# Where an MLP begins and ends: moved loads and squares, another product order, a scaling placed behind the next sum

## The chip, the cores and the metric

The kernel runs on one core of one Trainium2 chip. The metric is the device time of one execution in microseconds (us). The core's engines are TensorE (PE in the profile; its weight loads are PEld), VectorE (DVE), ScalarE (ACT), GpSimd (POOL) and SyncE (SP). SP, ACT and POOL also issue DMAs.

## The reference

One layer of a hybrid encoder on 512 rows of width 1024, in float32: two kinds of attention, a cross attention, then the part that matters here, an MLP with 4096 hidden columns, and a final normalisation.

```
h = h + concat(fox_out, rec) @ w_out
h = h + memory_cross_attention(rmsnorm(h), rmsnorm(mem), ...)
u = rmsnorm(h) @ w1            # (512, 1024) @ (1024, 4096)
h = h + square(relu(u)) @ w2   # (512, 4096) @ (4096, 1024)
out = rmsnorm(h)
```

## The kernel before

The last part of the kernel is the MLP. Its 4096 hidden columns are cut into 8 groups of 512 (`NG`). Within a group each matrix product, up (`u`, with `w1`) and down (`d`, with `w2`), is a 2 x 2 block product made of seven smaller products instead of eight; they are named "1" to "7". Their inputs are sums and differences of blocks. Only the last down group is done plainly, one block of 128 rows and one half of the columns at a time (`first_half`, steps "y", then `last_block`).

Each float32 operand is split into a high part in a rounded format and a low part that holds the rest, and each product is three matmuls: high x high, high x low, low x high. For weights the split (`prep`, through `split_of`) is one ScalarE instruction (line 163) and one VectorE instruction (line 165) for each block; the results `whu`/`wlu` and `whd`/`wld` live in rings of four buffers, so a split waits until the product four places earlier has been computed.

An up product (`up`) is 24 matmuls of 256 columns. Products "1", "6", "7", "4" add into one PSUM bank (`uU`, a pool with a single buffer), and "2" and "5", "3" into others (`uY`). As the bank is added to again, the running value is copied out to `h` by ScalarE (line 1350) behind "1", "6" and "5"; "7" can't begin to add until "6" is copied, and "1" of the next group can't begin until "4" has been read by its relu (`c`, line 1355). A down product (`down`) is 12 matmuls of 512 columns into the banks `U`, `Y` or `V`, and `add_to` (VectorE, line 1409) adds a finished bank, scaled with the row's factor `r2`, into `acc`, the residual of each block of 128 rows. `r2` comes from `row_scales`: four ScalarE squares of `acc` (128 x 1024 each, `aj`) and three tiny VectorE instructions.

The raw weights are loaded by SP (`load_raw`), block by block, into five slots for up (`uq`, `uk`, `us`) and five for down (`wq`, `dk`), by the roles a1, b1, a2, b2, c1. Sums of raw blocks are made by POOL's adding DMAs (`add_raw`) and, for up's c1, by VectorE. `begin` starts this for group 0, `behind` continues it behind each split.

The order of work: TensorE's instructions stay in the order of the text. The other engines' queues are ordered by a scheduler, which takes what is ready by its own clock, with the order of the text as priority. `tc.keep_in_program_order(x)` pins an instruction behind the one traced before it on its engine. The list `steps` sets which product comes when: all up products, with the down products slipped in from step 7 on; at the end the last down products alternate with the steps "y".

The end: for each of four row blocks, `last_block` makes the second half's products (12 matmuls, the last block's in two pieces), sums them into `acc` (VectorE), squares them (ScalarE, line 1460), makes the row's factor on POOL (`fe`, line 1463, and `fr`, line 1488) and scales the two halves by it, one on ScalarE (line 1489) and one on VectorE (line 1491); then both go out by DMA. `fa` (POOL, line 1486) is the first half multiplied by the final gain ahead of its factor.

Of the kernel before, what the change touches and what calls it, by code (L numbers as in the profile page):

```python
# [12 lines left out]
AF = mybir.ActivationFunctionType  # L13
ALU = mybir.AluOpType
# [3 lines left out]
S = 512  # L18
NT = S // P
D = 1024  # L20
KC = D // P
M = 256
WT = 256
# [4 lines left out]
EPS = 1e-6  # L28
# [14 lines left out]
def emit(  # L43
# [22 lines left out]
    te, ve, ac, gp = nc.tensor, nc.vector, nc.scalar, nc.gpsimd  # L66
# [26 lines left out]
    def s4(shape, name, dt=F32):  # L93
        return s4p.tile([P] + shape, dt, tag="s4", name=name)

    def k4(shape, name, dt=F32):
        return k4p.tile([P] + shape, dt, tag="k4", name=name)

    def q2(name, dt=R):
        return q2p.tile([P, 2, S], dt, tag="q2", name=name)  # L100
# [4 lines left out]
    def t2(name, dt=F32, shape=(S,)):  # L105
        return t2p.tile([P] + list(shape), dt, tag="t2", name=name)

    def sm(n, name):
        if n > 8:
            return s3p.tile([P, n], F32, tag="s3", name=name, padded_shape=[P, 32])  # L110
        return smp.tile([P, n], F32, tag="sm", name=name, padded_shape=[P, 8])

    def mm(name, shape=(S,)):
        return mmp.tile([P] + list(shape), F32, tag="mm", name=name)
# [7 lines left out]
    def tr(name, shape=(S,)):  # L122
        return trp.tile([P] + list(shape), F32, tag="tr", name=name)
# [25 lines left out]
    NG = DFF // HG  # L149
# [174 lines left out]
    mhalf = cp.tile([P, 8], F32, name="mhalf")  # L324
# [36 lines left out]
    for half in range(2):  # L361
        mkf = t2(f"mkf{half}", F32, (6, 64))
        gp.memset(mkf, 1.0)
        for li, m in enumerate(mlev[:-1]):
            v = mkf[:, li, :].rearrange("p (b m) -> p b m", m=m)
            nb = 64 // m
            o = half * m
# [538 lines left out]
    for n in range(len(units) + LAG):  # L906
        if n < len(units):
            p, tb, j = units[n]
# [39 lines left out]
    def hTc(c):  # L948
        return hT[c // 2][:, c % 2, :]
# [122 lines left out]
    acc = []  # L1072

    def to_tok(c):
        ps = tr(f"ht{c}")
        for tb in range(NT):
            te.transpose(ps[:, tb * P : (tb + 1) * P], hTc(c)[:, tb * P : (tb + 1) * P], ident)
        for tb in range(NT):
            d, s_ = acc[tb][:, c * P : (c + 1) * P], ps[:, tb * P : (tb + 1) * P]
            if tb % 2 == 0:  # L1080
                ac.activation(d, s_, AF.Copy)  # L1081
            else:
                ve.tensor_copy(d, s_)
# [100 lines left out]

    units, unit_q, keys = {}, deque(), []
    PRODUCTS = {"u": ("1", "2", "5", "6", "7", "3", "4"), "d": ("1", "2", "6", "5", "7", "3", "4")}
    RAW = {"1": "a1", "2": "b1", "6": "a1", "5": "c1", "7": "a2", "3": "b2", "4": "b1"}
    QUAD = {"a1": (0, 0), "a2": (0, 1), "b2": (1, 1), "b1": (1, 0)}
    slots = {}

    def quadrant(kind, g, role):
        r, c = QUAD[role]
        if kind == "u":
            a = w1[r * S : (r + 1) * S, g * HG + c * HS : g * HG + (c + 1) * HS]
        else:
            a = w2[g * HG + r * HS : g * HG + (r + 1) * HS, c * S : (c + 1) * S]
        return a.rearrange("(k p) n -> p k n", p=P)

    def parts_of(kind):
        return 4 if kind == "u" else 2  # L1200

    def load_raw(kind, g, role, source=None):

        if g >= NG:
            return
        slot = slots[kind, role]
        nc.sync.dma_start(slot.rearrange("p (k n) -> p k n", k=parts_of(kind)), quadrant(kind, g, source or role))

    def add_raw(kind, to, of):
        k = parts_of(kind)  # L1210
        src = of if of is not None and not isinstance(of, str) else slots[kind, of].rearrange("p (k n) -> p k n", k=k)
        gp.dma_start(slots[kind, to].rearrange("p (k n) -> p k n", k=k), src, accum_op=ALU.add)  # L1212

    def seven(kind, g):
        return g < (NG if kind == "u" else NG - 1)

    def first_sums(kind, g):

        if not seven(kind, g):
            return  # L1220
        if kind == "u":
            ve.tensor_tensor(slots[kind, "c1"], slots[kind, "a1"], slots[kind, "a2"], ALU.add)
            add_raw(kind, "a2", "b2")
        else:
            load_raw(kind, g, "c1", "a1")
# [5 lines left out]
    def second_sum(kind, g):  # L1231
        if kind == "d" and seven(kind, g):
            add_raw(kind, "a2", quadrant(kind, g, "b2"))

    def begin(kind):
        for role in ("a1", "b1", "a2", "b2"):
            load_raw(kind, 0, role)
        second_sum(kind, 0)
        first_sums(kind, 0)

    def behind(kind, g, name):

# [18 lines left out]
    def prep(kind, g, name):  # L1261
        raw = slots[kind, RAW[name] if seven(kind, g) else name]
        if seven(kind, g) and name == "4":
# [16 lines left out]
            prep(*unit_q.popleft())  # L1280
        return got

    ups = [("u", g, n) for g in range(NG) for n in PRODUCTS["u"]]
    downs = [("d", g, n) for g in range(NG - 1) for n in PRODUCTS["d"]]
    steps = []
    for i, step in enumerate(ups):
        steps.append(step)
        if i in (7, 9, 10, 12, 13, 15, 16) or i >= 18:
            steps.append(downs.pop(0))
    steps += downs[:2]  # L1290
    for i in range(NT):
        steps += [("y", NG - 1, str(i)), *downs[2 + i : 3 + i]]
    last_keys = [("d", NG - 1, n) for n in ("b1", "a1", "b2", "a2")]
    for key in steps:
        if key[0] != "y":
# [6 lines left out]
    def first_units():  # L1302

        ws = [wrp.tile([P, UK * UW], F32, tag="wr", name=f"us{i}")[:, 0:D] for i in range(2)]
        qs = [q2(f"uq{i}", F32).rearrange("p a b -> p (a b)") for i in range(2)]
        for role, slot in zip(("a1", "b1", "a2", "b2", "c1"), (*qs, k4([D], "uk"), *ws)):
            slots["u", role] = slot
        begin("u")
        for _ in range(2):
            prep(*unit_q.popleft())  # L1310

# [14 lines left out]
    wq = [ap_.tile([P, 4, D], F32, tag="act", name=f"wq{j}") for j in range(2)]  # L1326
    for role, slot in zip(("a1", "b1", "a2", "b2", "c1"), (*[wq[0][:, i, :] for i in range(4)], k4([D], "dk"))):
        slots["d", role] = slot
    begin("d")
    sqs = {(g, j): wq[1][:, g % 2 * 2 + j, :].rearrange("p (i n) -> p i n", i=2) for g in range(NG) for j in range(2)}  # L1330
    comb, hbs, held, banks = {}, {}, {}, {}

# [62 lines left out]

    r2 = cp.tile([P, 2, NT], F32, name="r2")

    def row_scales():
        ms = sm(NT, "ms2")
        for tb in range(NT):  # L1400
            junk = s4([D], f"aj{tb}")
            ac.activation(junk, acc[tb], AF.Square, scale=1.0 / 32.0, accum_out=ms[:, tb : tb + 1])
        ve.tensor_scalar(ms, ms, 1.0, EPS, op0=ALU.mult, op1=ALU.add)
        ve.reciprocal(r2[:, 0, :], ms)
        ve.tensor_scalar(r2[:, 1, :], r2[:, 0, :], -1.0, None, op0=ALU.mult)

    def add_to(ps, tb, cs, sign=1):
# [45 lines left out]
    sums, outs = {}, {}  # L1453
# [17 lines left out]
        if tb < 2:  # L1471
            squares(tb, slice(0, S))

    def last_block(tb, pieces):

        a = acc[tb]
        for n, ns in enumerate(pieces):
            ps = mm(f"y1{tb}_{ns.start}")[:, ns]
            plain_down(ps, tb, 1, ns)
            cs = slice(S + ns.start, S + ns.stop)  # L1480
            add_to(ps, tb, cs)
            squares(tb, cs, n == len(pieces) - 1)
        o, part = outs[tb], sums[tb][-1]
        h0, h1 = slice(0, S), slice(S, D)
        ag = t2(f"fa{tb}")
        gp.tensor_tensor(ag, a[:, h0], gfin[:, h0], op=ALU.mult)
        r = sm(1, f"fr{tb}")
        gp.tensor_tensor(r, part, mhalf[:, 0:1], op=ALU.pow)
        ac.activation(o[:, h0], ag, AF.Identity, scale=r)
        ac.dma_start(out[tb * P : (tb + 1) * P, h0], o[:, h0])  # L1490
        ve.scalar_tensor_tensor(o[:, h1], a[:, h1], r, gfin[:, h1], op0=ALU.mult, op1=ALU.mult)
        nc.sync.dma_start(out[tb * P : (tb + 1) * P, h1], o[:, h1])

    parts = deque()
    for n, (kind, g, name) in enumerate(steps):
        while parts and sum((a, b) in hbs for _, a, b in steps[n:] if _ == "d") < 2:
            hidden_part(*parts.popleft())
        if kind == "y":
            first_half(int(name))
            continue  # L1500
        (up if kind == "u" else down)(g, name)
        if (kind, g, name) == ("u", 0, "1"):
            to_tok(KC - 1)
            row_scales()
        if (kind, g, name) == ("d", NG - 2, "4"):
            while unit_q:
                prep(*unit_q.popleft())
        if (kind, g, name) == ("u", NG - 1, "3"):
            for k in range(2, 4):
                hidden_plain(g, k)  # L1510
        if (kind, name) == ("u", "4"):
            if g < NG - 1:
                parts.extend((g, m) for m in PRODUCTS["d"])
            else:
                for k in range(2):
                    hidden_plain(g, k)
    for tb in range(2, NT):
        squares(tb, slice(0, S))
    gfin = wrp.tile([P, UK * UW], F32, tag="wr", name="gfin")[:, 0:D]
    gp.dma_start(gfin, final_norm_g.partition_broadcast(P))  # L1520
    for tb in range(NT):
        last_block(tb, [slice(0, S)] if tb < NT - 1 else [slice(0, WT), slice(WT, S)])


# [26 lines left out]
```

## Time and profile before

| | |
|---|---|
| median of 3 runs | 783.56 us (782.96 to 784.21) |
| profiled execution, its own time | 782.28 us |
| its span in the profile | 780.4 us |
| TensorE busy | 759.8 us, 97% of the span |
| VectorE, ScalarE, GpSimd busy | 549.8, 432.0, 181.7 us |
| mean granted TensorE clock | 0.993 of full speed |
| MLP's first matmul, last matmul (start) | 445.6 us, 771.54 us |

The span is what the profiler saw from the first to the last instruction; the execution's own time is 1.9 us more. Row starts in the timeline are in us from the span's start, followed by the duration in us, the engine, the line, the operation, output<-input, and in brackets the idle time ahead of it with what ended it. A busy engine is not necessarily the bound, and idle time matters only on the chain that ends last.

### The profile page before, as it was taken

The page shows a single profiled execution, that of the slowest core. Times are in us where ns is not written, and L with a number is a line of the kernel's source. Part 1 is how long each engine was busy: PE and PEld are TensorE (multiplying, and loading weights), DVE is VectorE, ACT ScalarE, POOL GpSimd, SP SyncE. Part 2 cuts the span into 40 slices and gives each one's busy share as a digit, 9 for nine tenths or more (in the row PEclk, how much of TensorE's full clock was granted, in tenths as well). Part 3 has the DMA queues.
Part 4 walks back from the last instruction along what each step waited for, and adds up shares of the span by engine and source line. Part 5 has one row for each costly group of instructions (what it writes and reads, how often), then busy time and mean ns, then how long its engine had stood idle before and what let it go on. Part 6 is the DMA issues. An engine that isn't in the chain of part 4 may idle for free.

```text
span 780.4 us, 12861 instructions
## 1 busy us (share of the span) xinstructions
PE 759.8 (97%) x4940; PEld 672.0 (86%) x4940; DVE 549.8 (70%) x876; ACT 432.0 (55%) x730; POOL 181.7 (23%) x265
## 2 busy tenths in 40 slices
PE   7999999999999999999999989999999999999995
PEld 5889998978989998888888888989999898989874
DVE  3736755687677746645557777859797988888973
ACT  3664555575565533335445586646565656565733
POOL 6105332423433104510000111111112121212022
PEclk8999999999999999999999999999999999999998
DMA  6642332234444353221143789697988888888602
GB/s 194 222 128 80 111 81 56 82 72 119 136 129 142 118 180 105 84 82 55 55 134 108 150 229 198 166 256 172 209 198 230 189 239 189 237 192 168 167 27 109
DMA packets 84223, 113.11 MB, mean 145 GB/s; under 512 B 4881, under 2 KB 62778, under 8 KB 84162
## 3 DMA queue, kind: packets, MB, share of 16 engines
q1 hardware_dynamic: 69890, 74.25, 30.1%
q0 software_dynamic: 11568, 35.15, 23.2%
q10 hardware_dynamic: 2704, 2.89, 1.1%
q8 instruction: 39, 0.64, 0.3%
q14 instruction: 22, 0.18, 0.1%
HBM read 88.14 MB, written 4.21 MB: 118 GB/s over the span
## 4 chain that ended last, share of the span: by engine, by line
PE 90%; DVE 4%; ACT 3%; issue 1%; POOL 1%; DMA 1%; ACTq 0%; POOLq 0%
PE uU L1345 4%; PE uU L1346 4%; PE uU L1347 4%; PE U L1437 3%; PE U L1438 3%; PE U L1439 3%; PE uY L1346 3%; PE uY L1345 3%; PE uY L1347 3%; PE xq L226 2%; PE xw L226 2%; PE xw L228 2%; PE xq L228 2%; PE xq L227 2%; PE xw L227 2%; PE wo L226 2%
## 5 line engine op out<-in xcount | busy, mean ns | idle before, releaser
L163 ACT ACTIVATE whd<-wq 128x1024 fp32r<-128x1024 f32 x39 | 41.3, 1058 | 45.7 <-DMA wq<-wq 15.3
L165 DVE TENSOR_TENSOR wld<-wq,whd 128x1024 fp32r<-128x1024 f32 x39 | 47.6, 1220 | 12.9 <-ACT whd L163 12.8
L1345 PE MATMUL uU<-x2s,whu 128*128 128x256 f32 x160 | 45.9, 287 | 5.2 <-ACT h L1350 3.7
L1347 PE MATMUL uU<-x2s,wlu 128*128 128x256 f32 x160 | 45.3, 283 | 0.0
L1437 PE MATMUL U<-whd,hb 128*128 128x512 f32 x112 | 43.9, 392 | 0.0
L1438 PE MATMUL U<-wld,hb 128*128 128x512 f32 x112 | 43.9, 392 | 0.0
L1439 PE MATMUL U<-whd,hb 128*128 128x512 f32 x112 | 43.6, 389 | 0.0
L1409 DVE SCALAR_TENSOR_TENSOR acc<-U,r,acc 128x512 f32<-128x512 f32 x56 | 40.3, 743 | 4.3 <-PE U L1439 4.2
L163 ACT ACTIVATE whu<-uq 128x1024 fp32r<-128x1024 f32 x28 | 29.6, 1057 | 23.0 <-PE uU L1346 9.6
L165 DVE TENSOR_TENSOR wlu<-uq,whu 128x1024 fp32r<-128x1024 f32 x28 | 34.1, 1219 | 4.8 <-ACT whu L163 4.7
L1345 PEld LDWEIGHTS uU<-x2s,whu 128*128 128x128 f32 x160 | 30.6, 191 | 7.5 <-ACT h L1350 4.1
L1346 PE MATMUL uY<-x2a,whu 128*128 128x256 f32 x128 | 36.2, 283 | 0.0
L1346 PE MATMUL uU<-x2a,whu 128*128 128x256 f32 x128 | 36.2, 283 | 0.0
L1346 PE MATMUL uU<-x2b,whu 128*128 128x256 f32 x128 | 36.2, 283 | 0.0
L1212 POOL DMA_DIRECT2D uk<-us x8 | 8.2, 1026 | 111.1 <-ACT acc L1081 85.7
L163 ACT ACTIVATE whu<-us 128x1024 fp32r<-128x1024 f32 x20 | 21.2, 1060 | 21.1 <-PE uU L1346 16.0
L165 DVE TENSOR_TENSOR wlu<-us,whu 128x1024 fp32r<-128x1024 f32 x20 | 24.4, 1222 | 10.2 <-ACT whu L163 8.6
L847 POOL TENSOR_SCALAR bi<-nF,Ft 128x128 f32<-128x128 f32 (+3 forms) x32 | 21.4, 670 | 42.6 <-PE pt L874 25.1
L1347 PEld LDWEIGHTS uU<-x2s,wlu 128*128 128x128 f32 x160 | 30.6, 191 | 0.0
L864 ACT ACTIVATE bi<-bi,mx 128x128 f32<-128x128 f32 (+3 forms) x32 | 17.9, 559 | 20.9 <-DVE mx L862 20.7
L1345 PE MATMUL uY<-x2s,whu 128*128 128x256 f32 x96 | 27.2, 283 | 0.0
L1347 PE MATMUL uY<-x2s,wlu 128*128 128x256 f32 x96 | 27.2, 283 | 0.0
(944 smaller groups left out, 2826.3 us busy)
## 6 DMA issues: line engine op xcount, KB each, us to landing
wq<-in_w_dram SPq DMA_DIRECT2D x31, 512.0 KB, 5.1
uq<-in_w_dram SPq DMA_DIRECT2D x12, 512.0 KB, 5.0
us<-in_w_dram SPq DMA_DIRECT2D x12, 512.0 KB, 5.9
wq<-wq POOLq DMA_DIRECT2D x11, 512.0 KB, 7.7
wq<-in_w_dram POOLq DMA_DIRECT2D x10, 512.0 KB, 8.9
uk<-in_w_dram SPq DMA_DIRECT2D x8, 512.0 KB, 6.7
dk<-in_w_dram SPq DMA_DIRECT2D x8, 512.0 KB, 4.0
uk<-us POOLq DMA_DIRECT2D x8, 512.0 KB, 6.6
```

The costliest lines, as they stand in the source:

```text
L163: ac.activation(hi, raw, AF.Copy)
L165: ve.tensor_tensor(lo, raw, f(hi), ALU.subtract)
L226: te.matmul(ps, wh, hi, start=n_ == 0, stop=False)
L227: te.matmul(ps, wh, lo, start=False, stop=False)
L228: te.matmul(ps, wl, hi, start=False, stop=n_ == KC - 1)
L1345: te.matmul(ps[:, i, :], whi[:, k, ws], xh, start=first_ and (k, i) == (0, 0), stop=False, skip_group_check=True)
L1346: te.matmul(ps[:, i, :], whi[:, k, ws], xl, start=False, stop=False, skip_group_check=True)
L1347: te.matmul(ps[:, i, :], wlo[:, k, ws], xh, start=False, stop=k == 3, skip_group_check=True)
L1409: ve.scalar_tensor_tensor(a, ps, r2[:, 0 if sign > 0 else 1, tb : tb + 1], a, op0=ALU.mult, op1=ALU.add)
L1437: te.matmul(ps, hi, whi[:, k, :], start=first_ and k == 0, stop=False, skip_group_check=True)
L1438: te.matmul(ps, hi, wlo[:, k, :], start=False, stop=False, skip_group_check=True)
L1439: te.matmul(ps, lo, whi[:, k, :], start=False, stop=k == 1, skip_group_check=True)
```

## The change

- `begin` is cut into three: `a1` and `b1`, then `a2` and `b2`, then the sums. Up calls the three one behind the other as before. Down's, which stood ahead of all products, come one each behind the first three steps.
- The first up group takes its products in the order 1, 2, 6, 5, 7, 3, 4 instead of 1, 2, 5, 6, 7, 3, 4.
- The four row squares come one each behind steps 2 to 5, each pinned behind what was traced before it on ScalarE; the rest of `row_scales` comes behind step 6. Before, all of it came behind step 0.
- Down products are slipped in behind steps 7, 8, 10, 12, 13, 15 and from 17 on, instead of 7, 9, 10, 12, 13, 15, 16 and from 18 on.
- At the end the order y0, "3", y1, "4", y2, y3 becomes y0, y1, "3", y2, "4", y3.
- `last_block` is taken apart. The four `fa` products are traced first. Then each block's sums and squares come ahead of the scaling of the block before it, and its factor behind that; the two scalings are pinned to that place on ScalarE and VectorE.

```diff
+    def products(kind, g):
+        return PRODUCTS["d" if (kind, g) == ("u", 0) else kind]
...
-    def begin(kind):
-        for role in ("a1", "b1", "a2", "b2"):
-            load_raw(kind, 0, role)
-        second_sum(kind, 0)
-        first_sums(kind, 0)
+    def begin(kind, n):
+        if n < 2:
+            for role in (("a1", "b1"), ("a2", "b2"))[n]:
+                load_raw(kind, 0, role)
+        else:
+            second_sum(kind, 0)
+            first_sums(kind, 0)
...
-    ups = [("u", g, n) for g in range(NG) for n in PRODUCTS["u"]]
+    ups = [("u", g, n) for g in range(NG) for n in products("u", g)]
...
-        if i in (7, 9, 10, 12, 13, 15, 16) or i >= 18:
+        if i in (7, 8, 10, 12, 13, 15) or i >= 17:
             steps.append(downs.pop(0))
     steps += downs[:2]
     for i in range(NT):
-        steps += [("y", NG - 1, str(i)), *downs[2 + i : 3 + i]]
+        steps += [("y", NG - 1, str(i)), *(downs[1 + i : 2 + i] if i else ())]
...
-    begin("d")
...
+    def row_squares(tb):
+        junk = s4([D], f"aj{tb}")
+        square = ac.activation(junk, acc[tb], AF.Square, scale=1.0 / 32.0, accum_out=ms2[:, tb : tb + 1])
+        tc.keep_in_program_order(square)
...
-    def last_block(tb, pieces):
+    def last_sums(tb, pieces):
...
+    def last_factor(tb):
+        rs[tb] = sm(1, f"fr{tb}")
+        gp.tensor_tensor(rs[tb], sums[tb][-1], mhalf[:, 0:1], op=ALU.pow)
+
+    def last_scale(tb):
+        o = outs[tb]
+        tc.keep_in_program_order(ac.activation(o[:, h0], ags[tb], AF.Identity, scale=rs[tb]))
         ac.dma_start(out[tb * P : (tb + 1) * P, h0], o[:, h0])
-        ve.scalar_tensor_tensor(o[:, h1], a[:, h1], r, gfin[:, h1], op0=ALU.mult, op1=ALU.mult)
+        tc.keep_in_program_order(ve.scalar_tensor_tensor(o[:, h1], acc[tb][:, h1], rs[tb], gfin[:, h1], op0=ALU.mult, op1=ALU.mult))
...
-        if (kind, g, name) == ("u", 0, "1"):
+        if n < 3:
+            begin("d", n)
+        if n == 0:
             to_tok(KC - 1)
+        if 2 <= n < 6:
+            row_squares(n - 2)
+        if n == 6:
             row_scales()
...
     for tb in range(NT):
-        last_block(tb, [slice(0, S)] if tb < NT - 1 else [slice(0, WT), slice(WT, S)])
+        ags[tb] = t2(f"fa{tb}")
+        gp.tensor_tensor(ags[tb], acc[tb][:, h0], gfin[:, h0], op=ALU.mult)
+    for tb in range(NT):
+        last_sums(tb, [slice(0, S)] if tb < NT - 1 else [slice(0, WT), slice(WT, S)])
+        if tb:
+            last_scale(tb - 1)
+        last_factor(tb)
+    last_scale(NT - 1)
```

More of the change, by code (lines that the diff above doesn't have):

```diff
@@ L1307, in first_units @@
             slots["u", role] = slot
-        begin("u")
+        for n in range(3):
+            begin("u", n)
         for _ in range(2):
@@ L1396, in emit @@
     r2 = cp.tile([P, 2, NT], F32, name="r2")
-    def row_scales():
[L1399 to L1404, printed above, removed]
+    ms2 = sm(NT, "ms2")
+    def row_squares(tb):
+        junk = s4([D], f"aj{tb}")
+        square = ac.activation(junk, acc[tb], AF.Square, scale=1.0 / 32.0, accum_out=ms2[:, tb : tb + 1])
+        tc.keep_in_program_order(square)
+    def row_scales():
+        ve.tensor_scalar(ms2, ms2, 1.0, EPS, op0=ALU.mult, op1=ALU.add)
+        ve.reciprocal(r2[:, 0, :], ms2)
         ve.tensor_scalar(r2[:, 1, :], r2[:, 0, :], -1.0, None, op0=ALU.mult)
@@ L1472, in first_half @@
             squares(tb, slice(0, S))
-    def last_block(tb, pieces):
-        a = acc[tb]
+    def last_sums(tb, pieces):
         for n, ns in enumerate(pieces):
@@ L1482, in last_block @@
             squares(tb, cs, n == len(pieces) - 1)
[L1483 to L1489, printed above, removed]
+    h0, h1 = slice(0, S), slice(S, D)
+    def last_factor(tb):
[4 more added lines that the diff above has]
+        tc.keep_in_program_order(ac.activation(o[:, h0], ags[tb], AF.Identity, scale=rs[tb]))
         ac.dma_start(out[tb * P : (tb + 1) * P, h0], o[:, h0])
-        ve.scalar_tensor_tensor(o[:, h1], a[:, h1], r, gfin[:, h1], op0=ALU.mult, op1=ALU.mult)
+        tc.keep_in_program_order(ve.scalar_tensor_tensor(o[:, h1], acc[tb][:, h1], rs[tb], gfin[:, h1], op0=ALU.mult, op1=ALU.mult))
         nc.sync.dma_start(out[tb * P : (tb + 1) * P, h1], o[:, h1])
@@ L1520, in emit @@
     gp.dma_start(gfin, final_norm_g.partition_broadcast(P))
+    ags, rs = {}, {}
     for tb in range(NT):
-        last_block(tb, [slice(0, S)] if tb < NT - 1 else [slice(0, WT), slice(WT, S)])
+        ags[tb] = t2(f"fa{tb}")
[6 more added lines that the diff above has]
+    last_scale(NT - 1)
 _INS = ['x', 'mem', 'norm_mix_g', 'w_in', 'fox_f_bias', 'hgrn_lb_logits', 'hgrn_norm_g', 'w_out', 'norm_x_g', 'norm_mem_g', 'w_xq', 'w_xkv', 'w_xo', 'norm_ff_g', 'w1', 'w2', 'final_norm_g']
```

## The prediction

> **What bounds the kernel now.** I read the page's busy times first, then TensorE's own waits, then each engine's timeline around those waits.
>
> ```profile
> PE 759.8 (97%) x4940; PEld 672.0 (86%) x4940; DVE 549.8 (70%) x876; ACT 432.0 (55%) x730; POOL 181.7 (23%) x265
> ```
>
> TensorE (PE) is busy for 97% of the span. The change removes no matmul, so it can win only what TensorE loses to waits, and what lies behind its last matmul. TensorE's waits (line, releaser: us in total, times, longest) between 380 and 560 us, and those from 545 us to the end:
>
> ```profile
> PE uU L1345 <- ACT h L1350: 3.7, 2, 2.2
> PE uU L1345 <- ACT c L1355: 1.5, 1, 1.5
> ```
> ```profile
> PE Y L1438 <- DVE wld L165: 1.3, 1, 1.3
> ```
>
> In the whole MLP TensorE waits four times: twice for ScalarE's copy `h`, once for ScalarE's relu `c`, once for VectorE's low weight part `wld`. The tail behind the last matmul is the fifth loss. Each is one term below. A gap is counted from where the next matmul would have started at the usual spacing (0.12 us in an up product, 0.23 us in a down product). A further 0.10 us is an estimate for the first matmul behind each gap: it takes 0.39 instead of 0.28 us in the rows below.
>
> **Term A, the first group's order and the row squares.** TensorE's timeline, then ScalarE's (ACT):
>
> ```profile
> 457.48 0.28 PE L1347 MATMUL uU<-x2b,wlu 128*128 128x256 f32 x1
> 459.93 0.39 PE L1345 MATMUL uU<-x2s,whu 128*128 128x256 f32 x1 [2.18 <-ACT h L1350]
> ```
> ```profile
> 450.77 0.59 ACT L1350 ACTIVATE h<-uU 128x512 f32<-128x512 f32 x1
> ...
> 455.80 1.04 ACT L1402 ACTIVATE aj<-acc 128x1024 f32<-128x1024 f32 x1
> ...
> 458.35 1.04 ACT L163 ACTIVATE whu<-uq 128x1024 fp32r<-128x1024 f32 x1
> 459.30 0.58 ACT L1350 ACTIVATE h<-uU 128x512 f32<-128x512 f32 x1
> ```
>
> Product "6" ended at 457.6, and "7" adds into the same bank, so it waits until "6" is copied out. That copy ran only at 459.30, behind a queue that the four row squares (`aj`; the last at 455.80) had pushed back. The loss is 459.93 - 457.60 = 2.33, with the 0.10 it is 2.43 us. In the new order "5" stands between "6" and "7": 24 matmuls at 0.12 = 2.88 us in another bank, and the copy of "6" has that time. The first square is pinned behind that copy, so no square stands ahead of it. The price of the new order is that "6" starts right behind "2", 24 x 0.12 before 454.72, at 451.84 ("5" ran from there to 454.72), and needs the copy of "1", which ended at 450.77 + 0.59 = 451.36. That leaves 0.48 us, and nothing in the change is put ahead of that copy. I take 2.43, the stall gone. Bounds: 1.39 (one split of 1.04 us ahead of a copy with its cover used up) and 2.43.
>
> The squares aren't removed: four times 1.04 us of ScalarE move into the next products. ScalarE has room there (columns: stretch, length, busy time of PE, PEld, DVE, ACT, POOL, then clock, DMA share, GB/s):
>
> ```profile
> 445.00:461.00 16.00, 13.82 (x115) 13.53 (x114) 11.36 (x22) 14.83 (x27) 1.19 (x1) 1.00 1.02 305
> 461.00:470.00 9.00, 7.83 (x66) 7.62 (x64) 7.25 (x9) 6.62 (x10) 2.25 (x3) 1.00 0.39 75
> ```
>
> ScalarE is full in the first stretch, 14.83 of 16, and has 2.4 us free in the second. The scales made from the squares are wanted only by the first down product's sum, behind "1" of group 1. So the squares cost nothing but in term B; without that cover a square costs its 1.04.
>
> **Term B, from the first group to the second.** "1" of group 1 takes the one bank that "4" of group 0 leaves, and waits for its relu:
>
> ```profile
> 468.55 0.28 PE L1347 MATMUL uU<-x2s,wlu 128*128 128x256 f32 x1
> 470.35 0.39 PE L1345 MATMUL uU<-x2s,whu 128*128 128x256 f32 x1 [1.52 <-ACT c L1355]
> ```
> ```profile
> 468.75 1.06 ACT L163 ACTIVATE whu<-uq 128x1024 fp32r<-128x1024 f32 x1
> 469.71 0.58 ACT L1355 ACTIVATE c<-uU 128x512 f32<-128x512 f32 x1
> ```
>
> It loses 470.35 - 468.67 = 1.68, with 0.10 it is 1.78 us. No product comes between the two after the change either. The floor is the relu alone: the matmuls end at 468.55 + 0.28 = 468.83, the relu takes 0.58, and a hand-over costs 0.06 (469.71 + 0.58 to 470.35) at each end: 469.53, a loss of 0.96 and a gain of 0.82. At the ceiling the last square, pinned behind the square of "3", and a split both stand ahead of the relu: 1.04 worse than now. I take the case between them, the last square a third to run when "4" ends, a loss of 1.3: gain 0.48.
>
> **Term C, the third group.** The new list of steps moves a down product from behind "5" to behind "6" in group 2 (and from "5" to "2" in group 1); from step 18 on both lists put one behind every up product.
>
> ```profile
> 521.18 0.28 PE L1347 MATMUL uU<-x2b,wlu 128*128 128x256 f32 x1
> 522.97 0.39 PE L1345 MATMUL uU<-x2s,whu 128*128 128x256 f32 x1 [1.52 <-ACT h L1350]
> ```
>
> Here too "6" and "7" stood back to back: 522.97 - 521.30 = 1.67, with 0.10 it is 1.77 us. A down product, 12 matmuls at 0.23 = 2.75 us, now covers the copy. Gain 1.77; lower bound 0.73, with a split of 1.04 ahead of the copy.
>
> **The loads of down, later and one by one.** Five loads on SP's queue and one adding load on POOL's move behind loads and sums for the up products of group 1. Now:
>
> ```profile
> 445.28 2.00 SPq L1207 DMA_DIRECT2D wq<-in_w_dram  x4
> ```
> ```profile
> 454.57 1.19 POOL L1212 DMA_DIRECT2D wq<-in_w_dram  x1 [13.58 <-DMA wq<-in_w_dram]
> 463.52 0.89 POOL L1212 DMA_DIRECT2D uk<-us  x1 [7.75 <-DVE wlu L165]
> ...
> 473.81 0.86 POOL L1212 DMA_DIRECT2D us<-uq  x1 [3.42 <-DMA uq<-uk]
> ```
>
> The adding load held POOL's queue for 13.58 us, and the sums of group 1 stand behind it; the first of them (463.52) then waited for VectorE, not for it. With `a2` and `b2` issued behind up's third load, an estimated 4 us later, the adding load moves to about 458.5, still ahead of 463.52. The input of "6" of group 1 is in place at 473.81; its two splits take 1.06 on ScalarE and 1.22 on VectorE (row in term D). That product starts about 467.4 ("1" of group 1) + three up products and two down products, 14.1, at 481.5, so 5 us are left. TensorE has no wait for a DMA now, and I cost this edit at nothing. Bounds: 0, and a loss of 4 if the whole delay came through.
>
> **Term D, plain products sooner.** TensorE, then VectorE (DVE):
>
> ```profile
> 745.37 0.40 PE L1437 MATMUL Y<-whd,hb 128*128 128x512 f32 x1
> 747.11 0.50 PE L1438 MATMUL Y<-wld,hb 128*128 128x512 f32 x1 [1.34 <-DVE wld L165]
> ```
> ```profile
> 745.83 1.22 DVE L165 TENSOR_TENSOR wld<-wq,whd 128x1024 fp32r<-128x1024 f32 x1
> ```
>
> The loss is 747.11 - 745.60 = 1.51, with 0.10 it is 1.61 us. The second plain product, with the same weights and hidden parts as the first, which ran just before, now comes first: 2.75 us, to 748.35, while the split ends at 747.05. Late next are the last two splits, which wait for the buffers that "3" and "4" free, one plain product later than now. "4" would end at 745.60 + 4 x 2.75 = 756.6, its buffer's splits take 2.28, to 758.9, and their weights are read from 756.6 + 1.5 x 2.75 = 760.7. So the gap goes, and none takes its place: 1.61. Bounds: 0 and 1.61.
>
> **Term E, scaling behind the next sum.** The tail, all engines:
>
> ```profile
> 771.54 0.28 PE L1451 MATMUL y<-whd7a,hb 128*128 128x256 f32 x1
> ...
> 772.69 0.75 DVE L1491 SCALAR_TENSOR_TENSOR fo<-acc,fr,gfin 128x512 f32<-128x512 f32 x1 [1.45 <-POOL fr L1488]
> ...
> 773.36 0.48 DVE L1409 SCALAR_TENSOR_TENSOR acc<-y,r,acc 128x256 f32<-128x256 f32 x1
> ...
> 774.54 0.29 POOL L1463 TENSOR_SCALAR fe<-fm,fe 128x1 f32<-128x1 f32 x1 [0.33 <-ACT fo L1460]
> 774.92 0.56 POOL L1488 TENSOR_TENSOR fr<-fe,mhalf 128x1 f32<-128x1 f32 x1
> 775.51 0.72 ACT L1489 ACTIVATE fo<-fa,fr 128x512 f32<-128x512 f32 x1 [1.13 <-POOL fr L1488]
> ```
>
> The matmuls end at T = 771.82, but the last sum ran 1.54 us later, behind the scaling of block 2, which had waited for its own factor. Without that the sum runs at T + 0.06, `fe` 1.18 behind it, `fr` 0.38 behind that, the last scaling 0.59 later: T + 2.21 instead of T + 3.69. Gain 1.48. Block 2's scaling, 0.75, now runs from T + 0.54 to T + 1.29, while ScalarE and POOL make the last factor; without that cover it costs 0.75. Bounds: 0.73 and 1.48.
>
> A VectorE scaling now runs beside POOL's small steps, which it did not before. The same POOL product, first beside a split on VectorE, then alone:
>
> ```profile
> 747.80 2.20 POOL L1486 TENSOR_TENSOR fa<-acc,gfin 128x512 f32<-128x512 f32 x1 [20.74 <-DVE acc L1409]
> 753.72 1.30 POOL L1486 TENSOR_TENSOR fa<-acc,gfin 128x512 f32<-128x512 f32 x1 [3.73 <-DVE acc L1409]
> ```
>
> It took 0.90 us more beside the split. The Trainium skill, "SBUF — State Buffer", section "Who interferes with whom", says that a VectorE instruction with two inputs in SBUF keeps out a GpSimd instruction that reads SBUF; these two rows agree with it. By that rule `fe`, due at T + 1.24, would wait for the scaling's end at T + 1.29, and the sum would be 0.05 us smaller.
>
> **Sum.** 2.43 + 0.48 + 1.77 + 1.61 + 1.48 = 7.77 us. The profiled execution took 782.28 us, so 774.5 by its own time. The median of the runs shown, 783.56, lies 1.28 higher, and the forecast is made against it: 783.56 - 7.77 = 775.8.
>
> **Rivals.**
> 1. The stalls stay in part (chance 0.17). ScalarE's queue is ordered anew, and a split or square of 1.04 us stands ahead of a copy or a relu. For it: such a split stood ahead of the copy in A (458.35) and of the relu in B (468.75). Against it: in A and C the copies get 2.75 to 2.88 us of cover. With nothing gained in B and one further place paid with 1.04 the gain is 6.25: 777.3.
> 2. The front's gain is eaten later (0.09). TensorE comes 4.7 us (A, B, C) earlier, but VectorE, 70% busy over the span, or the loads can't follow. Against it: TensorE has one wait in all behind 545 us, so it is what the others follow. Only D and E stay, 3.1 us: 780.5.
> 3. The tail collides (0.07). Block 2's scaling delays POOL's last factor, or takes VectorE ahead of it, by its whole 0.75: 776.5. It needs that scaling to start late. Its own factor is due at about T - 0.2 (its matmuls end 24 x 0.12 before T; then the chain above, 0.5 longer for the double width), so it can start in time.
> 4. Slower (0.03), by POOL's queue. The adding load waits at its head for the later loads, and the sums of group 1 behind it come too late for "6" of group 1. It takes effect once these sums are 5 us later than now, and the time before is reached another 7.8 us on. The adding load can slip by 9 us before it meets 463.52, so the point is 454.57 + 9 + 12.8 = 476.4. At 479 the time is 786.2. No load in the profile is that late.
>
> That the scheduler issues the loads as early as now would change no term, and belongs to the forecast.
>
> **How the numbers follow.** The forecast has 0.62, a smaller gain of some other kind 0.02. A measurement of this kernel tells 0.2%, some 1.6 us, from no change. The range begins at 774.0 (B at its floor, 0.34 better, and 1.5 for the spread of runs, which is 1.25 in the three shown) and reaches to 779.3, beyond rivals 1 and 3 (0.62 + 0.17 + 0.07 = 0.86) and short of rival 2. Faster takes the forecast and rivals 1 to 3, 0.95, less 0.02 for a rival 2 that takes D and E along; same 0.04, slower 0.03.
>
> **What would show it.** Right: no wait of TensorE for `h` between 445 and 530 us, one of about 1 us for `c` ahead of group 1, none for `wld` near 740, and the last scaling about 2.2 us behind the last matmul. Wrong: a wait for `h` at product "6" (the 0.48 us), a wait for `wq` or a POOL sum between 465 and 500, a new wait between 545 and 735, or the last `fe` later than 1.4 us behind the last matmul.

## The result and the profile after

| | median, us | range | ratio to before, 95% interval |
|---|---|---|---|
| before, same chip | 783.56 | 782.75 to 786.21 (6 runs) | |
| changed | 777.2 | 774.89 to 779.25 (6 runs) | 0.9915 [0.989, 0.9941] |
| profiled execution of the changed kernel | 775.98 | span 774.3 | |

The change makes the kernel 6.4 us faster. The forecast was 775.8, range 774.0 to 779.3. Measured once more, beside the kernel before once more, it took 776.49 against 783.6.

The busy times of the changed kernel, then TensorE's waits from 380 to 560 us and from 545 us to the end (line, releaser: us in total, times, longest):

```profile
PE 758.6 (98%) x4940; PEld 671.2 (87%) x4940; DVE 549.8 (71%) x876; ACT 431.1 (56%) x730; POOL 181.3 (23%) x265
```
```profile
PE uU L1351 <- ACT c L1361: 1.2, 1, 1.2
```
```profile
PE uU L1351 <- ACT c L1361: 2.4, 3, 1.3
```

Both waits for `h` and the one for `wld` are gone. The wait for `c` ahead of group 1 is still there, and three waits for `c` are new in the list. TensorE's timeline of the changed kernel shows all four:

```profile
466.55 0.39 PE L1351 MATMUL uU<-x2s,whu 128*128 128x256 f32 x1 [1.15 <-ACT c L1361]
...
575.14 0.39 PE L1351 MATMUL uU<-x2s,whu 128*128 128x256 f32 x1 [1.27 <-ACT c L1361]
...
615.29 0.39 PE L1351 MATMUL uU<-x2s,whu 128*128 128x256 f32 x1 [0.54 <-ACT c L1361]
...
655.50 0.39 PE L1351 MATMUL uU<-x2s,whu 128*128 128x256 f32 x1 [0.60 <-ACT c L1361]
```

Counted as in the prediction (from where the matmul would have started at the usual spacing, without the extra 0.10), the gaps are 1.31, 1.42, 0.70 and 0.76, together 4.19. Before they were 2.33, 1.68, 1.67 and 1.51, together 7.19.

The tail of the changed kernel, behind its last matmul:

```profile
766.96 0.28 PE L1460 MATMUL y<-whd7a,hb 128*128 128x256 f32 x1
767.28 0.48 DVE L1418 SCALAR_TENSOR_TENSOR acc<-y,r,acc 128x256 f32<-128x256 f32 x1 [0.95 <-PE y L1460]
767.68 0.74 DVE L1501 SCALAR_TENSOR_TENSOR fo<-acc,fr,gfin 128x512 f32<-128x512 f32 x1
...
768.47 0.29 POOL L1472 TENSOR_SCALAR fe<-fm,fe 128x1 f32<-128x1 f32 x1 [1.14 <-ACT fo L1469]
768.85 0.56 POOL L1495 TENSOR_TENSOR fr<-fe,mhalf 128x1 f32<-128x1 f32 x1
...
769.44 0.75 DVE L1501 SCALAR_TENSOR_TENSOR fo<-acc,fr,gfin 128x512 f32<-128x512 f32 x1 [1.02 <-POOL fr L1495]
```

The matmuls end at T = 767.24. The last sum now runs ahead of block 2's scaling, and the last scaling starts at T + 2.20 instead of T + 3.69.

Where the 6.1 us of span went: the MLP's first matmul starts at 444.57 instead of 445.57, so 1.0 us lies ahead of everything the change touches (kernels whose text is the same up to there start it anywhere from 444.57 to 447.19). From that matmul to the last scaling it is 324.87 instead of 329.94 us, a gain of 5.07: 3.00 in gaps, 1.49 in the tail, and 0.58 spread over spacings without a gap of 0.3 us (0.54 of it were three short waits of the kernel before, shown below). The terms A, C, D and E had promised 7.29, and B brought 0.37; the three new waits took 2.88 back, 3.18 with their three slow first matmuls. That leaves 4.48, which is what gaps and tail show (3.00 + 1.49).

### What the new waits are

POOL's timeline of the changed kernel around the group of the second wait. The instructions are adding DMAs; the bracket is the time for which POOL was idle ahead of each:

```profile
543.44 1.21 POOL L1216 DMA_DIRECT2D wq<-in_w_dram  x1 [0.72 <-DMA wq<-in_w_dram]
556.71 1.20 POOL L1216 DMA_DIRECT2D dk<-in_w_dram  x1 [12.06 <-DMA dk<-in_w_dram]
557.44 1.39 POOL L1216 DMA_DIRECT2D wq<-wq  x1
```

ScalarE's timeline behind it:

```profile
567.42 1.06 ACT L163 ACTIVATE whd<-wq 128x1024 fp32r<-128x1024 f32 x1 [5.37 <-DMA wq<-wq]
568.39 1.04 ACT L163 ACTIVATE whu<-uq 128x1024 fp32r<-128x1024 f32 x1
...
573.57 1.04 ACT L163 ACTIVATE whu<-uq 128x1024 fp32r<-128x1024 f32 x1
574.52 0.57 ACT L1361 ACTIVATE c<-uU 128x512 f32<-128x512 f32 x1
```

Down's sum a1 += a2 (`wq<-wq`) is issued at 557.44, directly behind an adding load of c1 (`dk`), for which POOL's queue had stood idle for 12.06 us, until that block's raw load landed. So the sum lands late, and ScalarE, whose next instruction is the split of that sum, idles 5.37 us. From 567.42 on ScalarE works without a pause through what has queued up, and the relu `c` comes at its end, at 574.52. TensorE can't begin the next group until `c` has read the bank.

ScalarE's waits of the kernel before, from 545 to 700 us, and its timeline at the same place, have the same wait (the last row is TensorE's):

```profile
ACT whd L163 <- DMA wq<-wq: 15.3, 4, 4.1
```
```profile
570.83 1.06 ACT L163 ACTIVATE whd<-wq 128x1024 fp32r<-128x1024 f32 x1 [3.21 <-DMA wq<-wq]
...
577.92 0.57 ACT L1355 ACTIVATE c<-uU 128x512 f32<-128x512 f32 x1
```
```profile
579.28 0.28 PE L1345 MATMUL uU<-x2s,whu 128*128 128x256 f32 x1
```

There the relu ended at 578.49 and TensorE wanted the bank at 579.28: a margin of 0.79 us. In the changed kernel TensorE would have arrived at 575.14 - 1.42 = 573.72, 5.56 us earlier, but the sum's split started only 3.41 us earlier (570.83 to 567.42). The difference, 2.15, less the margin of 0.79, is 1.36, and the gap is 1.42.

Ahead of groups 5 to 7 the kernel before had no margin at all. ScalarE's timeline of the kernel before, then TensorE's, with its weight loads (PEld):

```profile
618.07 0.58 ACT L1355 ACTIVATE c<-uU 128x512 f32<-128x512 f32 x1
...
697.11 0.58 ACT L1355 ACTIVATE c<-uU 128x512 f32<-128x512 f32 x1
```
```profile
618.70 0.19 PEld L1345 LDWEIGHTS uU<-x2s,whu 128*128 128x128 f32 x1 [0.35 <-ACT c L1355]
618.70 0.39 PE L1345 MATMUL uU<-x2s,whu 128*128 128x256 f32 x1
...
697.74 0.19 PEld L1345 LDWEIGHTS uU<-x2s,whu 128*128 128x128 f32 x1 [0.41 <-ACT c L1355]
697.74 0.38 PE L1345 MATMUL uU<-x2s,whu 128*128 128x256 f32 x1
```

The relu ends 0.05 us ahead of the matmul, which is no more than a hand-over, and the matmul comes 0.08 and 0.14 us later than the usual spacing and is a slow first one. Ahead of group 6, at 658.17, it is 0.02 late. With 0.10 for each first matmul the three come to 0.54 us. They are too short for the list of waits, which has only `wld` there. So the late sums already set TensorE's pace in these groups, and nothing was left for a TensorE that comes earlier.

### The profile page after: what moved, and what is told of

It reads as the page before. It is cut to its first block, busy times and chain, and to the rows that moved or that the text cites. A ratio compares the mean times of both kernels' runs of the same rounds, so it can differ in the third digit from the quotient of the medians.

```text
span 774.3 us, 12863 instructions
## 1 busy us (share of the span) xinstructions
PE 758.6 (98%) x4940; PEld 671.2 (87%) x4940; DVE 549.8 (71%) x876; ACT 431.1 (56%) x730; POOL 181.3 (23%) x265
```

## The experiments

All are timed in five rounds beside the kernel before on the same chip (783.6 to 784.1). The gaps are TensorE's, read from each timeline.

**1. The changed kernel again, and a pin on POOL's queue.** My theory: the order of POOL's queue makes the new waits. In the text the sum a1 += a2 comes ahead of the adding load of c1; the scheduler had put it behind. The pin keeps the text's order:

```diff
-        gp.dma_start(slots[kind, to]..., src, accum_op=ALU.add)
+        return gp.dma_start(slots[kind, to]..., src, accum_op=ALU.add)
...
-            add_raw(kind, "c1", quadrant(kind, g, "a2"))
+            tc.keep_in_program_order(add_raw(kind, "c1", quadrant(kind, g, "a2")))
```

> The changed kernel once more, unchanged, beside the others of this chip. Its profile showed four waits of TensorE for the relu c, one ahead of group 1 (1.31 us of gap) and three new ones ahead of groups 4, 5 and 6 (1.42, 0.70, 0.76). If these belong to the order of the queues, they stand here again at the same places with sums within 0.5 us, and the time is 775 to 779 us. If they were an accident of one execution, they are elsewhere or gone.

> The changed kernel with one more pin: on POOL, the adding load of c1 from memory stays behind the sum a1 += a2, as in the text, instead of ahead of it. Theory P (POOL's queue): a1 += a2 stood behind the adding load, which waited 12 us for its raw load; so the split of d '6' came late on ScalarE, and the relu behind it. Then a1 += a2 is issued about 5 us earlier (near 552 instead of 557.4), ScalarE's wait for wq<-wq of 4 to 5 us falls to under 1, the three new waits of TensorE go, and the time falls by 2.4 to 3 us against the changed kernel. Theory Q (the DMA engines are full, busy share 0.9 and more in that stage, and the sums land late whatever their order): ScalarE still waits 3 us or more, the waits of TensorE keep at least 2 us in sum, and the time is within 1 us of the changed kernel.

The changed kernel again: 776.49 (775.67 to 778.29), 0.9897 [0.9873, 0.9921]. Its gaps are 1.31 ahead of group 1 and then 0.67, 1.73 and 1.15 at about 537, 617 and 658 us: the new waits stand ahead of groups 3, 5 and 6 instead of 4, 5 and 6, with the same releaser. Together they are 3.55 instead of 2.88, so two of the three places stay, but neither the third nor the sum, which was expected within 0.5. With the pin: 774.09 (772.81 to 774.53), 0.9865 [0.9841, 0.9889]. POOL's timeline of the pinned kernel, then ScalarE's, then TensorE's waits from 380 us to the end:

```profile
542.57 1.21 POOL L1216 DMA_DIRECT2D wq<-in_w_dram  x1 [1.88 <-DMA wq<-in_w_dram]
555.79 0.91 POOL L1216 DMA_DIRECT2D wq<-wq  x1 [12.01 <-DVE wld L165]
556.36 1.58 POOL L1216 DMA_DIRECT2D dk<-in_w_dram  x1
```
```profile
564.41 1.06 ACT L163 ACTIVATE whd<-wq 128x1024 fp32r<-128x1024 f32 x1 [0.62 <-PE U L1448]
...
573.75 0.57 ACT L1361 ACTIVATE c<-uU 128x512 f32<-128x512 f32 x1
```
```profile
PE uU L1351 <- ACT c L1361: 1.2, 1, 1.2
```

The sum now goes first, as soon as VectorE has read the block that it overwrites. Counted from each kernel's first MLP matmul it is issued 3.4 us earlier (555.79 - 446.31 = 109.48 against 557.44 - 444.57 = 112.87). ScalarE's split no longer waits for a DMA but for TensorE, all three new gaps are gone, and only the one ahead of group 1 is left. In every later group the relu now ends 1.12 or 1.13 us before TensorE's matmul. The runs also lie closer together, within 1.7 us instead of 2.6 for the changed kernel on the same chip (4.4 in the first measurement). So the order of POOL's queue is shown to be the cause.

**2. Down's loads put back ahead of all products**, the rest of the change kept. The rival theory was that the later loads make the sums late.

```diff
+    for n in range(3):
+        begin("d", n)
...
-        if n < 3:
-            begin("d", n)
```

> The changed kernel with down's first loads all at once ahead of the products again, as before the change; everything else as changed. Theory L (the later loads put the whole chain of raw sums 2 us later, and this shows as the three new waits): the waits go or halve, and the time falls by 1.5 to 3 us. Theory P: the waits stay, since the order on POOL is the same in the later groups; the time is within 1 us of the changed kernel, and the loads' move is worth nothing by itself.

776.85 (775.86 to 779.33), 0.9905 [0.9881, 0.9928]: as the changed kernel. A gap of 1.74 stands at 576.44, and ScalarE waits four times for the sum, 17.6 us in all. The one new gap is less than the changed kernel's 2.88 and 3.55, as the rival would have it, but the time did not fall by the 1.5 to 3 us that the rival needs, and the sums are as late. Moving the loads neither costs nor brings anything that can be measured here, and the rival falls.

**3. Only the end of the change** (terms D and E: the plain products sooner, and `last_block` taken apart as in the change), with the old front. Against the kernel before, its line in the list of steps is:

```diff
-        steps += [("y", NG - 1, str(i)), *downs[2 + i : 3 + i]]
+        steps += [("y", NG - 1, str(i)), *(downs[1 + i : 2 + i] if i else ())]
```

> Only the end is changed: plain products sooner and the scaling behind the next sum (terms D and E). Loads, squares, product order and list of steps as before the change. By the prediction's terms it gains 1.61 + 1.48 = 3.1 us against the kernel before: 780.5 by its median. The waits for h and c at the front stay as before (3.7 and 1.5 us), and there are no new waits ahead of groups 4 to 6, as the front's stalls give the raw sums their time. Rival: if the new waits came from the end's part of the change, they stand here.

780.95 (778.95 to 784.15, 12 runs), 0.9961 [0.9944, 0.9978], 2.65 us faster. The wait for `wld` is gone, the old front has its old gaps (2.34, 1.68, 1.68), and TensorE's timeline has a new one of 1.50:

```profile
699.75 0.39 PE L1353 MATMUL uU<-x2s,whu 128*128 128x256 f32 x1 [1.34 <-ACT c L1363]
```

That is the wait for `c` again, ahead of group 7, in a kernel whose TensorE comes no earlier; the kernel before had no margin at this place. So the late sums can stop TensorE without the front's gain too; that gain makes the waits likelier and larger, but isn't the whole cause.

This execution also lost some 1.5 us at a place that no term names. Behind the old gap of 2.34 the granted clock fell to 0.50 of full speed, and 16 matmuls came at 0.21 us each instead of 0.12. The kernel before has the same gap without that. Its stretch comes second (columns as in the prediction):

```profile
460.00:462.00 2.00, 2.00 (x11) 2.00 (x11) 2.00 (x2) 0.38 (x1) 0.34 (x1) 0.50 0.22 63
```
```profile
460.00:462.00 2.00, 2.00 (x17) 2.00 (x18) 1.97 (x3) 1.35 (x2) 0.00 (x0) 1.00 0.89 168
```

Of the four profiled executions with that gap, two have the fall, this one and the one without A and B in experiment 5; of the ten without the gap none has it between 445 us and the last matmul. So term A may bring more than its gap in some executions. Why the clock falls in some and not in others isn't shown.

**4. The pin alone on the kernel before.** If the old kernel loses something to POOL's queue in some executions, the pin helps it too.

> The kernel before with the pin on POOL as its only change. Theory P says that the late sums stay hidden there, 0.8 us from a wait, as long as the front's stalls give them time: no less than 783.0 us, within 0.6 of the kernel before, and its four waits as they were. If the sums cost it something in most executions, it is faster by 1 us or more and its runs lie closer together.

782.49 (781.8 to 783.31, 12 runs), 0.9985 [0.9975, 0.9994], with the gaps of before (2.33, 1.68, 1.67, 1.54). That is below the 783.0 that the theory allowed if the sums stay hidden: they cost the old kernel something. Its profiled execution shows 0.54 us of it, the three short waits ahead of groups 5 to 7, where with the pin the relu ends 1.13 us early. That other executions lose more than this is argued and not shown. With the pin in both, the change is worth 9.51 - 1.26 = 8.25 us, each taken against the kernel before on its own chip, where the prediction's sum was 7.77.

**5. Terms A, B, C and E one at a time, in the pinned kernel** (774.09), where no wait that wanders between groups blurs the comparison. Each run takes one part of the change back.

Without the order, `PRODUCTS[kind]` stands again for `products(kind, g)`; without the squares' move, all four come behind step 0 without pins; A and B together are these two. Without C:

```diff
-        if i in (7, 8, 10, 12, 13, 15) or i >= 17:
+        if i in (7, 9, 10, 12, 13, 15, 16) or i >= 18:
```

Without E, the tail is the old one again, block by block, and its scalings have no pins:

```diff
     for tb in range(NT):
         last_sums(tb, ...)
-        if tb:
-            last_scale(tb - 1)
+        ags[tb] = t2(f"fa{tb}")
+        gp.tensor_tensor(ags[tb], acc[tb][:, h0], gfin[:, h0], op=ALU.mult)
         last_factor(tb)
-    last_scale(NT - 1)
+        last_scale(tb)
```

> The changed kernel with the pin on POOL, but the first group's product order and the place of the row squares as before (term A off). The wait for h at '7' of group 0 is back with 2.3 us of gap, and the one for c ahead of group 1 with 1.7 instead of 1.3. By terms A and B it is slower than the pinned kernel by 2.43 + 0.4 = 2.8 us: 776.9.

> The changed kernel with the pin on POOL, but the list of steps as before (term C off). The wait for h in group 2 is back with a gap of 1.67 us, and nothing else changes: slower than the pinned kernel by 1.8 us, 775.9. If the down product's other place in group 1 matters by itself, another gap stands in group 1.

> The changed kernel with the pin on POOL, but the end in the old manner: each block's scaling ahead of the next block's sum, unpinned, the products with the gain one by one (term E off). The last scaling starts 3.7 us behind the last matmul instead of 2.2, and the time is 1.5 us above the pinned kernel: 775.6. If what is gained there is lost in the output's DMA, the span behind the last scaling is longer with the change, and the difference is under 0.7 us.

> The changed kernel with the pin on POOL, but the first group's product order as before ('5' ahead of '6'); the row squares stay one by one in their new places. '6' and '7' stand back to back, so the copy alone costs a gap of 0.84 us at least and up to 1.9 with a split ahead of it: 775.0 to 776.0. If it is 0 the order was not needed; if it is 2.3 the squares were not what made the copy late.

> The changed kernel with the pin on POOL, but all four row squares behind step 0 and unpinned, as before; the new product order stays. If the order alone does term A, the gap ahead of '7' of group 0 is under 0.3 us, since '5' covers 2.88 us of ScalarE's queue, and the time is within 0.5 us of the pinned kernel. If the squares were the cause, a gap of 1 to 2 us stands at '7' or ahead of group 1: 775.1 to 776.1.

| taken back | median, us | ratio to before | more than 774.09 | what the trace has back |
|---|---|---|---|---|
| A and B | 777.42 (777.36 to 777.92) | 0.9919 [0.9903, 0.9936] | 3.3 | gaps of 2.33 (`h`) and 1.68 (`c`) |
| C | 775.23 (774.61 to 776.76) | 0.9895 [0.9875, 0.9915] | 1.1 | a gap of 1.68 (`h`) |
| E | 775.22 (774.62 to 776.02) | 0.9891 [0.9874, 0.9908] | 1.1 | span's end 8.89 behind the last matmul instead of 7.01 |
| only the order | 775.29 (774.81 to 775.95) | 0.9896 [0.9881, 0.9912] | 1.2 | a gap of 1.68 (`h`) instead of none |
| only the squares | 774.13 (773.67 to 774.41) | 0.9879 [0.9862, 0.9896] | 0.0 | gaps of 0.38 (`h`) and 1.16 (`c`) instead of 1.31 (`c`) |

The traces give back the gaps that terms A, B and C had named. Without E the last scaling starts 3.96 us behind the matmuls' end instead of 2.20, so E is 1.76 here, where the term had 1.48. By medians C and E come out 0.6 and 0.8 us smaller than by the trace (1.68 and 0.10 for C, 8.89 - 7.01 for E); each ratio's interval reaches 1.2 to 1.9 us to either side, so a difference of two kernels can't tell 0.8 from nothing; the gaps can. Without A and B the profiled execution also has the fall of the clock of experiment 3, some 1.5 us, which stands in none of the gaps. The rows of the last two runs tell the order from the squares. TensorE's timeline with only the order taken back:

```profile
458.95 0.39 PE L1351 MATMUL uU<-x2s,whu 128*128 128x256 f32 x1 [1.52 <-ACT h L1356]
...
469.00 0.39 PE L1351 MATMUL uU<-x2s,whu 128*128 128x256 f32 x1 [1.15 <-ACT c L1361]
```

and with only the squares taken back:

```profile
458.00 0.39 PE L1351 MATMUL uU<-x2s,whu 128*128 128x256 f32 x1 [0.23 <-ACT h L1356]
...
467.90 0.38 PE L1351 MATMUL uU<-x2s,whu 128*128 128x256 f32 x1 [1.01 <-ACT c L1361]
```

The new order does nearly all of term A by itself: the squares in their old place cost 0.38 at `h` (under 0.3 was expected), and the wait for `c` is then 0.15 shorter, so their move is worth 0.2 us of gaps and nothing in the time.

**6. What is left ahead of group 1.** ScalarE's timeline of the changed kernel has the last square right ahead of the relu:

```profile
464.88 1.04 ACT L1408 ACTIVATE aj<-acc 128x1024 f32<-128x1024 f32 x1
...
465.92 0.58 ACT L1361 ACTIVATE c<-uU 128x512 f32<-128x512 f32 x1
```

Two trials, both with the pin on POOL: the squares one step later, and the first group's relu of "4" on VectorE.

```diff
-        if 2 <= n < 6:
-            row_squares(n - 2)
+        if 3 <= n < 7:
+            row_squares(n - 3)
```
```diff
-        if of is None:
+        if of is None and g == 0:
+            ve.tensor_scalar(c, ps, 0.0, None, op0=ALU.max)
+        elif of is None:
             ac.activation(c, ps, AF.Relu)
```

> The changed kernel with the pin on POOL, and the four row squares one step later (behind steps 3 to 6), so that the last one stands behind the relu c of product '4' and not ahead of it. If that square alone makes the one wait that is left (1.31 us of gap ahead of group 1), the gap falls to 0.8 or 0.9, the relu alone, and the time to 773.6 us (0.5 less than with the pin alone). Rival: the hidden part of the first down product, which now stands behind the last square, comes late, and a wait of TensorE at that product takes the gain back: 774.1 to 774.6.

> The changed kernel with the adding loads in the pinned order on POOL's queue, and the relu of the first group's product "4", the first one that the products of group 1 wait for, put on VectorE (a maximum with 0) instead of ScalarE. In the pinned kernel (774.1) TensorE waits 1.31 us ahead of group 1, and a row square of 1.04 stands right ahead of that relu on ScalarE. If ScalarE's queue makes this wait, VectorE, which needs about 0.7 us for such a read, can begin at once: the wait falls to 0.85 to 0.95 us and the time to 773.7. The rival: VectorE is itself behind a split of 1.22 us at that moment; the wait stays at 1.2 us or more and the time at 774.1.

With the squares a step later: 774.31 (773.59 to 774.34), 0.9876 [0.9857, 0.9895], the gap again 1.31. Another square, the third, had taken the fourth's place ahead of the relu, so this run says nothing on what the relu costs alone. With the relu on VectorE: 773.17 (772.81 to 773.84, 4 runs), 0.9862 [0.9844, 0.9881]. Its VectorE timeline, then TensorE's:

```profile
466.45 0.69 DVE L1361 TENSOR_SCALAR c<-uU 128x512 f32<-128x512 f32 x1 [0.39 <-PE uU L1353]
```
```profile
467.20 0.39 PE L1351 MATMUL uU<-x2s,whu 128*128 128x256 f32 x1 [0.78 <-DVE c L1361]
```

The gap falls from 1.31 to 0.95, since VectorE was idle when the bank was ready. So ScalarE's queue makes the part of the wait that was expected of it, and no more: the 0.95 that is left is the last matmul's own end (0.16), the read (0.69) and a hand-over on each side (0.04 and 0.06). The step of 0.36 us in the gap can be read in the trace; in the times it can't be told from the pinned kernel (0.9862 against 0.9865). These two, the pinned kernel and this one, beat both kernels of the case.

## Why the prediction was right, and where it was not

- **Term A** (2.43): right. No wait for `h` in the first group. Of the two causes that it named, the cover that the new order gives decides; that no square stands ahead of the copy matters little (0.38).
- **Term B** (0.48): right in its mechanism and nearly in its size. The loss left is 1.31 + 0.10 = 1.41 where 1.3 was forecast, a gain of 0.37. The last square did stand ahead of the relu, and the relu started 1.04 behind the square's start.
- **Terms C and D** (1.77 and 1.61): right, both waits are gone, and the trace has C's 1.68 again when the old list of steps is put back. D was measured only together with E.
- **The loads** (0): right. The adding load of a2 went from 454.57 to 456.55, less late than the 458.5 expected, and nothing waited for it; put back they give the same time.
- **Term E** (1.48): right, 3.69 - 2.20 = 1.49. Rival 3, the collision in the tail, did not come. `fe` started at T + 1.23, 0.05 behind the end of VectorE's scaling (767.68 + 0.74 = 768.42, `fe` at 768.47). The Trainium skill's rule ("SBUF — State Buffer", section "Who interferes with whom") would have it wait for that end, and the row agrees with it; but the plain chain gave T + 1.24, so the row can't tell the two apart, and either way it costs no more than the 0.05 given for it. One reading of the prediction is off: the second `fa`, called alone, ran beside a VectorE sum (754.03, 0.75 us) that takes one of its blocks from PSUM. Its two rows compare a split with such a sum, not with an idle VectorE.
- **The sum** (7.77): 6.4 by the medians, 1.4 short of it. In the profiled execution all terms together come to 7.66 (7.29 and B's 0.37), the new waits take 3.18 of that, and 0.58 in other spacings and 1.0 ahead of the MLP, both of which no term had named, make up for part. So the time came close to the forecast partly by luck: the terms less the new waits are 4.48 us in that execution. One of the prediction's own signs of being wrong came true, a new wait between 545 and 735, three times over. With the pin, which takes the new waits away, the change is worth 8.25.
- **The step that failed** stands under rival 2: "TensorE has one wait in all behind 545 us, so it is what the others follow." The count came from the list of waits, which leaves short ones out: TensorE also waited for `c` ahead of groups 5 to 7, by 0.02 to 0.14 us, and followed ScalarE there. And that the bound engine doesn't wait shows that the others are in time, not by how much. The profile of before held the answer in views that the prediction doesn't use: ScalarE's 15.3 us of waits for a sum's DMA, ahead of relus that had 0.79 us to spare ahead of group 4 and nothing ahead of the next three. Rival 2 named the right place ("the front's gain is eaten later") with the wrong cause and size: neither VectorE nor the loads were too slow, one queue had two of its entries in a bad order, and some 2.9 of the front's 4.7 us were lost, not all. Rival 1's time, 777.3, is close to the measured 777.2 by accident: its copies and relus late in A, B and C weren't what cost the time.

Two things stay open. Why the raw load of c1 lands when it does, and so why a wait moves from one group to another between executions, wasn't traced to its source. And the 1.0 us by which the MLP began earlier in the profiled execution is taken as scatter, from starts of other kernels, and wasn't tested.

## What to carry to other kernels

When the engine that bounds a kernel is made earlier, list not only its own waits but those of the engines that feed it, and for each the margin between its end and the moment at which it is needed; a margin smaller than the gain (here 0.79 us and then none, against 4.7) is a term of the sum. A first matmul that comes 0.1 us late behind another engine can be, as here, the sign that this engine sets the pace. In a queue that is served in order, an instruction that waits for a load holds up whatever was put behind it: look for long idle times ahead of a DMA issue, and for what is issued right behind it. A product put between two that share a bank covered a copy whole, where clearing ScalarE's queue ahead of it brought 0.65 of 2.33 us.

## What the hardware showed beside that

- A sum by an adding DMA takes long from its issue to its use: a1 += a2 was issued at 557.44 and its split on ScalarE, which waited for nothing else, began at 567.42, 10.0 us later; in the pinned kernel it was 8.6 (555.79 to 564.41), there with the split waiting for TensorE at the end. The median from issue to landing is 7.7 us in the changed kernel's list of DMA issues (instructions, KB each, us):

```profile
wq<-wq POOLq DMA_DIRECT2D x11, 512.0 KB, 7.7
```

  In the five kernels without the pin this median is 7.7 to 7.9 us, in the nine with it 5.0 to 7.3. So the sum not only starts sooner behind the pin, it also tends to land faster; why isn't shown.

- The same DMAs seem to make the times scatter: with POOL's order pinned the runs of the changed kernel lay within 1.7 us instead of 2.6, and the kernel before, 782.2 to 785.5 on that chip, within 1.5 with the pin.
